# One PSUM bank of the differential attention taken from another pool: the transposed results' bank in a hybrid decoder layer

## The chip, the cores and the metric

The kernel runs on one core of one Trainium2 chip. The metric is the device time of one execution in microseconds; the time of a version is the median of its runs.

## The reference, cut to what matters

One decoder layer on x of 512 tokens by 2048 features, all in float32. A normalised h is multiplied by one wide matrix `w_in`. Its columns feed four heads of gated linear attention (GLA), a gate for them, and four heads of differential attention:

```python
# diff_attention, per head and block of 128 query rows; two score maps c = 0, 1
s = einsum('bqhcd,bkhcd->bhcqk', qi, k) * scale + bias      # ALiBi, causal
p = softmax(s, axis=-1)
a = p[:, :, 0] - lam * p[:, :, 1]
o = einsum('bhqk,bkhe->bqhe', a, v)
# token_mixer
o_b = rmsnorm(o_b, diff_norm) * (1.0 - lambda_init)
return concatenate([o_a, o_b]) @ w_o                         # o_a: the GLA heads, gated
```

Then come a residual, a second norm, and a gated MLP with a causal convolution of width 3 on one branch. `w_in`, `w_o` and the MLP's matrices are what most of the work is spent on.

## The kernel before, in words

**Split products.** Each weight block of 128 x 1024 floats (a granule, `granule`, L128) is loaded, copied by ScalarE into a rounded high half (L137), and VectorE makes the low half by subtraction (L138). Three matmuls per pair of operands (high by high, high by low, low by high) make one product. The halves live in three slots of `ring`.

**Projection units.** `InUnit` (L696) computes one 512-column piece of `w_in` as a block product with seven partial products, the segments x0, z0, y0, z1, x1, y1 and y2. A segment is two granules of 24 matmuls. A segment that begins a sum opens a PSUM bank with `bank(psm)` (L729): x0 opens the bank "y", z0 the bank "z", x1 the bank "x". Bank y stays open from x0 to y2 of its unit, bank z from z0 to z1, bank x for x1 alone. ScalarE or VectorE takes the sums out (L757, L762, L771 and L793 on ScalarE; L776, L782 and L787 on VectorE). The next unit's x0 stands ahead of the old unit's y2, so two banks y can be open at a time. There are ten units (L865 to L872); the last two make the gate of the GLA heads (L810: a product, a sigmoid and another product, L819 to L821, then a store to `ogd`).

**PSUM.** Eight banks of 128 x 512 floats are in two pools of four: `psm` for the block products and `psa` for everything else (L61, L62). `bank()` without an argument takes one of `psa` (L77).

**The attention as filling.** GLA and differential heads are generators. After each granule's products a unit calls `step()` (L84), which advances the first live generator, 0.75 steps per granule. One step i of `diff_heads` (L667 to L688) issues, in this order, for five different blocks of 128 query rows:

- `store(i-5)` (L655): two TensorE transposes of the finished rows `on` into a bank `ob` (L659), a ScalarE copy into `dst` (L661), and a DMA to `dstd`, issued from ScalarE's queue (L662);
- `values(i-3)` (L642): the products with `dvt`, the head's v (L646), then a square on ScalarE (L649), the norm's factor on GpSimd (L144, L146) and the scaled rows `on` on VectorE (L652);
- `fetch_v` of the next head, when a head has ended (L604, one buffer);
- `probs(i)` (L606): two score banks (L614), then VectorE and ScalarE in turn: bias (L616), maximum (L618, L620), exponential (L622), reciprocal (L624, L628), scaling (L629) and difference (L630);
- `turn(i-2)` (L633): transposes of the probabilities into a bank (L637), copied out by ScalarE (L639).

So a step opens five banks of `psa`: one in `store`, one in `values`, two in `probs`, one in `turn`. The rows `jk`, `on` and `dst` share three SBUF buffers (`row_tile`, L339).

**The order.** In this stretch no order is written out by hand. A planner in the framework (Tile) takes the instructions in the order in which the program states them as priorities, simulates the engines, gives each tile a free buffer of its pool and fixes each engine's order; a tile whose buffer is in use makes its first writer wait for the last user. Each engine then runs its own list strictly in that order.

The call sites that drive the attention (`InUnit.run`, L723, calls `step()` at L750) are outside the functions printed here:

```python
            there[after[i - 1][0]] = after[i - 1][1]   # L911: a head's q and k are now there
        pace[0] = 0.75                                   # L913: steps of filling per granule
            drain()                                      # L921: in the last unit, all that is left
```

Of the kernel before, what the change touches and what calls it, by code (L numbers as in the profile page):

```python
# [35 lines left out]
def hybrid_layer(ctx: ExitStack, tc: tile.TileContext, x, attn_pre_norm, w_in, w_alpha_up, b_alpha,  # L36
# [24 lines left out]
    psm = ctx.enter_context(tc.tile_pool(name="psm", bufs=4, space=PSUM))  # L61
# [15 lines left out]
    def bank(pool=None):  # L77
        return (pool or psa).tile([P, 512], F32, name="bank", tag="bank")
# [260 lines left out]
    def row_tile(name):  # L339
        return mx.tile([P, GDV], F32, name=name, tag="jk", bufs=3)  # L340
# [245 lines left out]
    def diff_heads():  # L586
# [67 lines left out]

        def store(n, on):  # L655
            h, qb = divmod(n, NT)
            ob = bank()
            for j in range(2):
                nc.tensor.transpose(ob[:, j * P:(j + 1) * P], on[:, j * P:(j + 1) * P], ident)  # L659
            o = row_tile("dst")  # L660
            act(o, ob[:, :2 * P], AF.Copy)  # L661
            nc.scalar.dma_start(out=dstd[h][:, :, qb * P:(qb + 1) * P], in_=o.rearrange("p (j c) -> p j c", j=2))  # L662
# [4 lines left out]
        for i in range(N + 5):  # L667
            h = i // NT
            if i < N and i % NT == 0:
                while there["diff"] <= h:  # L670
                    yield
                if h not in qs:
                    fetch(h)
                    yield
                    yield
            if i - 5 in summed:
                store(i - 5, summed.pop(i - 5))
            if i - 3 in turned:
                summed[i - 3] = values(i - 3, turned.pop(i - 3))
            if i % NT == 2 and i > NT and h < DH:  # L680
                fetch_v(h)
            if i < N:
                scored[i] = probs(i)
                if i % NT == 3 and h + 1 < there["diff"]:
                    fetch(h + 1)
            if i - 2 in scored:
                turned[i - 2] = turn(i - 2, scored.pop(i - 2))
            yield  # L688
# [968 lines left out]
```

## Time and profile before

| what | value |
|---|---|
| median of 3 runs | 2109.35 us (2107.22 to 2112.05) |
| the profiled execution's own time | 2105.36 us |
| its span, first to last instruction | 2103.7 us |
| mean granted TensorE clock | 0.998 |
| stores of the differential heads (L659) | first at 428.9 us, last at 594.3 us |

The profile gives, per instruction, its engine, its start and its duration; what an engine waited for ahead of it is inferred from semaphores and shown as `[idle <-releaser]`. A row such as `PE bank L637 <- ACT dst L661: 2.3, 2, 1.6` says that TensorE's instructions of line 637, which write a bank, stood waiting 2.3 us in all, 2 times, 1.6 at most, until ScalarE's instruction of line 661, which writes `dst`, had ended. PE is TensorE, PEld its weight loads, ACT ScalarE, DVE VectorE, POOL GpSimd and SP the queue that issues most loads; a `q` behind a name is an engine's instruction queue.

### The profile page before, as it was taken

The page shows a single profiled execution, that of the slowest core. Times are in us where ns is not written, and L with a number is a line of the kernel's source. Part 1 is how long each engine was busy: PE and PEld are TensorE (multiplying, and loading weights), DVE is VectorE, ACT ScalarE, POOL GpSimd, SP SyncE. Part 2 cuts the span into 40 slices and gives each one's busy share as a digit, 9 for nine tenths or more (in the row PEclk, how much of TensorE's full clock was granted, in tenths as well). Part 3 has the DMA queues.
Part 4 walks back from the last instruction along what each step waited for, and adds up shares of the span by engine and source line. Part 5 has one row for each costly group of instructions (what it writes and reads, how often), then busy time and mean ns, then how long its engine had stood idle before and what let it go on. Part 6 is the DMA issues. An engine that isn't in the chain of part 4 may idle for free.

```text
span 2103.7 us, 35572 instructions
## 1 busy us (share of the span) xinstructions
PE 2061.9 (98%) x14449; PEld 1900.6 (90%) x14449; DVE 1508.8 (72%) x1802; ACT 1000.8 (48%) x1306; POOL 286.9 (14%) x306
## 2 busy tenths in 40 slices
PE   7999999999999999999999999999999999999997
PEld 6799999999898889899999999999999878787786
DVE  5967777676662255986777777777777778888877
ACT  4544444455652233454554554555455554444443
POOL 0112122322110000011111111110111111110100
PEclk9999999999999999999999999999999999999999
DMA  5478887878874244448668577667776876775653
GB/s 210 123 185 183 196 184 176 185 172 193 195 201 174 96 151 160 140 102 196 149 149 195 144 162 185 143 159 171 173 160 172 248 210 155 210 184 147 172 168 140
DMA packets 280696, 358.60 MB, mean 170 GB/s; under 512 B 14592, under 2 KB 221876, under 8 KB 278612
## 3 DMA queue, kind: packets, MB, share of 16 engines
q1 hardware_dynamic: 191380, 259.85, 36.9%
q0 software_dynamic: 84800, 94.38, 29.5%
q8 instruction: 113, 1.85, 0.4%
q10 hardware_dynamic: 4352, 2.10, 0.3%
q14 instruction: 51, 0.42, 0.1%
HBM read 311.72 MB, written 44.56 MB: 169 GB/s over the span
## 4 chain that ended last, share of the span: by engine, by line
PE 50%; issue 19%; POOL 2%; DVE 2%; DMA 2%; ACT 1%; POOLq 0%; DVEq 0%; ACTq 0%
PE bank L1247 10%; PE bank L1246 10%; PE bank L1248 10%; PE bank L191 3%; PE bank L193 3%; PE bank L192 3%; PE bank L175 1%; PE bank L173 1%; PE bank L174 1%; PE bank L1349 1%; PE bank L1350 1%; PE bank L1348 1%; POOL rt L1194 1%; POOL raw L1194 1%; PE bank L746 1%
## 5 line engine op out<-in xcount | busy, mean ns | idle before, releaser
L138 DVE TENSOR_TENSOR ring<-raw,ring 128x1024 fp32r<-128x1024 f32 x315 | 383.5, 1222 | 280.7 <-ACT ring L137 280.4
L137 ACT ACTIVATE ring<-raw 128x1024 fp32r<-128x1024 f32 x315 | 333.2, 1060 | 506.8 <-PE bank L1247 110.4
L1246 PE MATMUL bank<-ah,ring 128*128 128x256 f32 x1280 | 353.3, 276 | 0.0
L1248 PE MATMUL bank<-ah,ring 128*128 128x256 f32 x1280 | 353.3, 276 | 0.0
L1247 PE MATMUL bank<-al,ring 128*128 128x256 f32 x1280 | 353.3, 276 | 0.0
L137 ACT ACTIVATE ring<-rt 128x1024 fp32r<-128x1024 f32 x221 | 233.4, 1060 | 252.1 <-PE bank L1247 158.5
L138 DVE TENSOR_TENSOR ring<-rt,ring 128x1024 fp32r<-128x1024 f32 x221 | 269.2, 1222 | 90.3 <-ACT ring L137 90.1
L1247 PEld LDWEIGHTS bank<-al,ring 128*128 128x128 f32 x1280 | 240.2, 188 | 0.1
L1246 PEld LDWEIGHTS bank<-ah,ring 128*128 128x128 f32 x1280 | 240.2, 188 | 0.1
L1248 PEld LDWEIGHTS bank<-ah,ring 128*128 128x128 f32 x1280 | 240.2, 188 | 0.0
L1349 PE MATMUL bank<-ring,ah 128*128 128x512 f32 x424 | 166.3, 392 | 5.6 <-DVE ring L138 5.6
L1350 PE MATMUL bank<-ring,al 128*128 128x512 f32 x424 | 165.2, 390 | 0.0
L1348 PE MATMUL bank<-ring,ah 128*128 128x512 f32 x424 | 159.0, 392 | 1.0 <-ACT ring L137 0.9
L191 PE MATMUL bank<-ring,ah 128*128 128x512 f32 x280 | 109.8, 397 | 1.9 <-ACT ring L137 1.9
L192 PE MATMUL bank<-ring,ah 128*128 128x512 f32 x280 | 110.2, 395 | 0.4 <-DVE ring L138 0.4
L193 PE MATMUL bank<-ring,al 128*128 128x512 f32 x280 | 109.2, 393 | 0.0
L1194 POOL DMA_DIRECT2D raw<-in_w_ffn_in_dram x40 | 51.2, 1308 | 395.0 <-DVE ring L138 395.0
L1349 PEld LDWEIGHTS bank<-ring,ah 128*128 128x128 f32 x424 | 79.6, 188 | 25.8 <-DVE ring L138 9.5
L1348 PEld LDWEIGHTS bank<-ring,ah 128*128 128x128 f32 x424 | 79.2, 188 | 20.2 <-ACT ring L137 3.7
L1194 POOL DMA_DIRECT2D rt<-in_w_ffn_in_dram x40 | 50.9, 1271 | 327.4 <-DVE ring L138 281.8
L1350 PEld LDWEIGHTS bank<-ring,al 128*128 128x128 f32 x424 | 79.6, 188 | 16.3
L746 PE MATMUL bank<-ring,ah 128*128 128x256 f32 x320 | 93.1, 291 | 0.0
(346 smaller groups left out, 5672.4 us busy)
## 6 DMA issues: line engine op xcount, KB each, us to landing
raw<-in_w_ffn_in_dram SPq DMA_DIRECT2D x96, 512.0 KB, 5.0
raw<-in_w_in_dram SPq DMA_DIRECT2D x56, 512.0 KB, 4.7
raw<-in_w_ffn_out_dram SPq DMA_DIRECT2D x48, 512.0 KB, 6.1
raw<-in_w_in_dram POOLq DMA_DIRECT2D x40, 512.0 KB, 7.1
rt<-in_w_ffn_in_dram SPq DMA_DIRECT2D x40, 512.0 KB, 5.5
rt<-in_w_ffn_in_dram POOLq DMA_DIRECT2D x40, 512.0 KB, 6.1
raw<-in_w_ffn_in_dram POOLq DMA_DIRECT2D x40, 512.0 KB, 6.7
raw<-in_w_o_dram SPq DMA_DIRECT2D x32, 512.0 KB, 3.8
```

The lines of the kernel that those rows point to most:

```text
L137: act(hi, raw, AF.Copy)
L138: tt(lo, raw, hi.bitcast(F32), ALU.subtract)
L191: mm(banks[t], ah[:, t, s, :], w[0][:, k, :], start=st, stop=False)
L192: mm(banks[t], ah[:, t, s, :], w[1][:, k, :], start=False, stop=False)
L193: mm(banks[t], al[:, t, s, :], w[0][:, k, :], start=False, stop=sp)
L1194: nc.gpsimd.dma_start(out=raws[g].rearrange("p (a b) -> p a b", a=self.a), in_=self.block(0, j, g), accum_op=ALU.add)
L1246: mm(o, wh, sh[:, :, kk, :], start=start and kk == 0 and n == 0, stop=False, **NOW)
L1247: mm(o, wh, sl[:, :, kk, :], start=False, stop=False, **NOW)
L1248: mm(o, wl, sh[:, :, kk, :], start=False, stop=kk == HK - 1, **NOW)
L1348: mm(b[j], sh[:, o:o + P], w[0][:, q, :], start=start and st == 0, stop=False, **NOW)
L1349: mm(b[j], sh[:, o:o + P], w[1][:, q, :], start=False, stop=False, **NOW)
L1350: mm(b[j], sl[:, o:o + P], w[0][:, q, :], start=False, stop=st == 3, **NOW)
```

## The change

`store` asks for its bank in `psm`, the pool of the block products, in place of `psa`. The transposes, the copy and the DMA are the same instructions. A step of the differential attention now opens four banks of `psa` and one of `psm`.

```diff
         def store(n, on):
             h, qb = divmod(n, NT)
-            ob = bank()
+            ob = bank(psm)
             for j in range(2):
                 nc.tensor.transpose(ob[:, j * P:(j + 1) * P], on[:, j * P:(j + 1) * P], ident)
             o = row_tile("dst")
```

## The prediction

> **What bounds the kernel now.** I read the page first, then the busy time by stage, the waits of the stretch with the stores, and the order of time on each engine where a wait stands.
>
> ```profile
> PE 2061.9 (98%) x14449; PEld 1900.6 (90%) x14449; DVE 1508.8 (72%) x1802; ACT 1000.8 (48%) x1306; POOL 286.9 (14%) x306
> ...
> 429.00:600.00 171.00, 164.84 (x1272) 155.56 (x1271) 109.34 (x200) 96.37 (x183) 38.67 (x47) 0.99 0.82 191
> ```
>
> TensorE is the bound: 98% of the span, and 164.84 of the 171 us from the first store to the last. The change adds and removes no instruction, so all that it can win in its own stretch is TensorE's idle time there, 171.00 - 164.84 = 6.2 us, and a slower clock behind it. Which part of the 6.2 us is a wait for a bank? The waits of 429 to 600 us (total, times, longest):
>
> ```profile
> DVE on L652 <- DMA dstd<-dst: 10.0, 4, 5.2
> ...
> PE bank L637 <- ACT dst L661: 2.3, 2, 1.6
> ...
> PE bank L646 <- DVE nm L620: 2.0, 1, 2.0
> ...
> PE bank L659 <- DVE s L616: 0.9, 1, 0.9
> ...
> PE bank L659 <- ACT aT L639: 0.2, 1, 0.2
> ```
>
> L637 (the transposed probabilities) needs nothing that L661 makes; it waits because L661 empties the store's bank, which is its own next one. L659 (the store) needs neither L616 nor L639; it waits for a score bank and for a transposed one to be emptied. These are the waits of a pool with five openings a step and four banks. In order of time on TensorE:
>
> ```profile
> 492.06 0.55 PE L637 MATMUL bank<-ident,s 128*128 128x128 f32 x3 [0.77 <-ACT dst L661]
> ...
> 544.62 0.55 PE L637 MATMUL bank<-ident,s 128*128 128x128 f32 x3 [1.55 <-ACT dst L661]
> ...
> 547.33 0.44 PE L659 MATMUL bank<-ident,on 128*128 128x128 f32 x2 [0.89 <-DVE s L616]
> ...
> 562.14 0.44 PE L659 MATMUL bank<-ident,on 128*128 128x128 f32 x2 [0.17 <-ACT aT L639]
> ...
> 565.54 0.67 PE L646 MATMUL bank<-dvt,aT 128*128 128x256 f32 x2 [2.01 <-DVE nm L620]
> ```
>
> The last one is named after a VectorE instruction that L646 doesn't need, but another thing ends just then. L646 here begins a new head, whose v was loaded late:
>
> ```profile
> 560.97 0.36 SPq L48 DMA_DIRECT2D ogd<-u  x1
> 561.42 0.57 SPq L48 DMA_DIRECT2D dvt<-dvd  x1
> ...
> dvt<-dvd SPq DMA_DIRECT2D x1, 512.0 KB, 4.0
> ```
>
> Issued at 561.42 and landed 4.0 us later is 565.42; L646 starts at 565.54. I read this wait as the DMA's, not a bank's.
>
> **The change part by part.**
>
> *What goes.* With four openings of `psa` a step, a bank comes round after a full step in place of four fifths of one, and `turn` no longer follows the store's copy. All four bank waits go: 0.77 + 1.55 + 0.89 + 0.17 = 3.38 us. What is late next at 544.62? The probabilities are old by then; behind the transposes the products need their granule's halves.
>
> ```profile
> 543.39 1.23 DVE L138 TENSOR_TENSOR ring<-raw,ring 128x1024 fp32r<-128x1024 f32 x1 [1.75 <-ACT ring L137]
> ...
> 545.93 0.28 PE L748 MATMUL bank<-ring,ah 128*128 128x256 f32 x1
> ```
>
> The low half is there at 543.39 + 1.23 = 544.62. Counting 24 products to a granule from 533.66 on, L748 at 545.93 is the first that uses it; moved up by 1.55 it would come at 544.38, so 0.24 us is given back. Left: 3.14 us.
>
> *What of it is given back later.* The 0.77 at 492 comes ahead of a long run of products without a wait, and I count it in full. The other 1.55 - 0.24 + 0.89 + 0.17 = 2.37 us lie ahead of the wait for v, and are worth something only if v lands earlier too. What sets v? SP issues it behind `ogd<-u`, whose data VectorE finishes at 560.94; that follows from here:
>
> ```profile
> 550.03 0.36 ACT L661 ACTIVATE dst<-bank 128x256 f32<-128x256 f32 x1
> 550.42 0.52 ACTq L662 DMA_DIRECT2D dstd<-dst  x1
> ...
> 554.85 0.48 DVE L652 SCALAR_TENSOR_TENSOR on<-bank,rs,dnb 128x256 f32<-128x256 f32 x1 [2.08 <-DMA dstd<-dst]
> ...
> 555.58 0.68 DVE L787 TENSOR_TENSOR u<-u,bank 128x512 f32<-128x512 f32 x1
> ...
> 560.25 0.69 DVE L821 TENSOR_TENSOR u<-u,op 128x512 f32<-128x512 f32 x1 [1.81 <-ACT u L820]
> ```
>
> VectorE stands 2.08 us until a store's DMA has given back a row buffer, and the unit's emptying (L787), the gate (L819, L820, L821), `ogd<-u` and v queue behind it. The store's transposes at 547.33 + 0.44 were done 2.3 us ahead of its copy at 550.03: the copy stands behind the exponentials in ScalarE's list, which wait for VectorE, not for TensorE. So if ScalarE's order stays, v lands at 565.4 whatever TensorE does, and TensorE waits there 2.01 + 2.37 = 4.4 us. Ends for this part: 0 and 2.37 us won. I take 0, for the row nearest to it (v's issue) says so.
>
> *The clock.* After that wait TensorE is slow:
>
> ```profile
> 562.00:566.00 4.00, 1.84 (x12) 1.64 (x13) 3.75 (x9) 3.30 (x5) 1.41 (x2) 1.00 0.95 305
> 566.00:570.00 4.00, 4.00 (x11) 2.31 (x11) 3.76 (x8) 2.06 (x8) 1.11 (x2) 0.59 0.42 132
> ```
>
> The columns are PE, PEld, DVE, ACT, POOL, then the granted clock. After 4 us with 1.84 busy the clock is 0.59 for 4 us, which costs (1 - 0.59) x 4 = 1.6 us. It is the one such dip from the first store to the last. If the wait shrinks or shifts, these 1.6 us are won; if it grows to 4.4, as much may be lost again. I take 0.
>
> The Trainium skill, "TensorE: Matmul & The Clock Gate", section "Why this matters for your kernels", asks for no idle gap of TensorE above some 3 us. By that rule the 2.01 us here would cost nothing more, and only the longer wait would; the row speaks against it, with a slow clock behind 2.01 us (its section "What's actually happening" has the activity judged over a window that runs freely, which a shorter gap can mostly fill, and that the row allows).
>
> *What is added.* `psm` gets 16 openings, each held from the transposes to the copy's end. What I can see of the four banks:
>
> ```profile
> 435.64 0.38 PE L659 MATMUL bank<-ident,on 128*128 128x128 f32 x2
> ...
> 437.62 0.28 PE L742 MATMUL bank<-ah,ring 128*128 128x256 f32 x1
> ...
> 437.93 0.36 ACT L661 ACTIVATE dst<-bank 128x256 f32<-128x256 f32 x1
> ...
> 438.44 0.69 DVE L776 TENSOR_TENSOR u<-bank,u 128x512 f32<-128x512 f32 x1
> ...
> 594.26 0.41 PE L659 MATMUL bank<-ident,on 128*128 128x128 f32 x2
> ...
> 596.51 0.28 PE L746 MATMUL bank<-ring,ah 128*128 128x256 f32 x1
> ...
> 599.05 0.37 ACT L661 ACTIVATE dst<-bank 128x256 f32<-128x256 f32 x1
> ...
> 599.79 0.68 DVE L776 TENSOR_TENSOR u<-bank,u 128x512 f32<-128x512 f32 x1
> ```
>
> At 437.62 x1 opens a bank while y is open, z isn't emptied until 439.13 and the store's bank would be held until 438.29: the fourth of four. At 596.51 it is the same, the store's held until 599.42 and z until 600.48. Nowhere did I find a fifth, so every opening has a bank that is free. Bounds: 0, and the time that the store's bank is still held where a product opens one: 438.29 - 437.62 = 0.67, 599.42 - 596.51 = 2.91, and a third at 498.59 of 0.32 (below): 3.9 us. Where a wait is added, all products queue behind it on TensorE. I take 0, for free banks are what the rows show.
>
> ```profile
> 498.59 0.47 PE L746 MATMUL bank<-ring,ah 128*128 128x256 f32 x1
> ...
> 498.55 0.36 ACT L661 ACTIVATE dst<-bank 128x256 f32<-128x256 f32 x1
> ```
>
> *Sum.* -0.77 us; against the profiled execution's own time 2105.36 - 0.8 = 2104.6. That run lies 4.0 us under the median, which stands for the kernel, so I put it on the median: 2109.35 - 0.8 = 2108.6.
>
> **The rivals.**
>
> *Faster: the stores move up.* Without a bank of `psa` to wait for, the planner may place L659, and with it L661, ahead of the step's exponentials. Then dst lands earlier, L652's wait (10.0 us in 4 times on VectorE) shrinks, and gate and v come earlier by the 2.08 us. TensorE wins the whole 3.14 us, and the dip of 1.6 us may go: -4.7, 2104.6 us. All idle time and the dip, 6.2 + 1.6 = 7.8, is the end: 2101.5. For it: the 10.0 us are real, and stand on the path to v. Against: in all three of the copies that I show in order (437.93, 550.03, 599.05) ScalarE came late for other reasons than the bank. Chance 0.22.
>
> *Slower: products wait for the store's copy.* If the planner, whose ScalarE may be ahead of the real one, gives an opening product the bank that a store has just left, TensorE stands until L661 has ended. It decides wherever the copy ends later than the product's turn comes, at the three places above: 3.9 us, with one more dip behind the 2.91 of 1.6 us. 3.9 + 1.6 - 0.8 = +4.7: 2114.1 us. For it: copies end up to 599.42 - 594.26 = 5.2 us after their transposes. Against: a fourth bank was free. The Trainium skill, "Perfetto Trace Analysis", section "Matmuls", wants independent groups to rotate through banks so that one is emptied beside the next one's matmuls; a foreign, slowly emptied tenant in that rotation is what it would warn of, and no row here shows one yet. Chance 0.27.
>
> *Nothing happens.* The planner's order stays and L637 finds another bank late, L639's or L616's: 2109.4 us. Chance 0.10, within the same verdict. The forecast itself has 0.41.
>
> **How the numbers follow.** A measurement of this kernel tells about 0.2%, 4.2 us, from no change. Faster: 0.22, and 0.02 of the forecast's tail: 0.24. Slower: 0.27. Same: the rest of the forecast and the case of nothing, 0.49. The range reaches from under the end of the faster case, 2101.5 less 1 us, 2100.5, to 2114.1 and the 2.7 us by which one run of before lay above its median: 2116.8.
>
> **What would show it.** Right: L637 no longer waits for L661, L659 for neither L616 nor L639; no product (L742 to L748) waits for L661; TensorE's wait ahead of the first L646 of the last head is longer than 2.01 us, behind a v that is issued near 561 us less 0.8. The faster rival shows as L661 ahead of L622 in ScalarE's order, less than 10.0 us of L652 waiting for dst, and no dip of the clock. The slower one shows as PE L742 or L746 waiting for ACT L661. I am wrong in the whole if the planner's new order moves time outside 429 to 600 us.

## The result and the profile after

| version | runs | median us | range us | ratio to the kernel before, with interval |
|---|---|---|---|---|
| before | 15 | 2109.20 | 2104.25 to 2114.40 | |
| changed | 15 | 2104.41 | 2100.50 to 2106.97 | 0.9979 (0.9970 to 0.9989) |
| changed, a second time | 12 | 2104.73 | 2100.67 to 2109.07 | 0.9984 (0.9973 to 0.9995) |

The change gains some 0.2%: 4.8 us by the first pair of medians, 2.4 us by the second (before: 2107.17 in 35 runs). That it is faster is clear of the noise in both comparisons; by how much is not, for the two intervals reach from 0.05% to 0.30%. The forecast was 2108.6, a gain of 0.8 us on the 2109.35 of before.

The profiled execution of the changed kernel took 2106.11 us (span 2104.4), 0.75 us *more* than that of before. Single executions of either kernel spread over more than 6 us, so the two profiles show which waits come and go, but not what the median does. First the stretch with the stores and its waits, as before:

```profile
429.00:600.00 171.00, 163.35 (x1269) 155.45 (x1268) 112.71 (x204) 100.05 (x192) 39.65 (x47) 0.99 0.84 198
```

```profile
ACT ah L150 <- DMA dt<-dstd: 9.4, 2, 7.9
...
PE bank L659 <- DVE on L652: 5.7, 1, 5.7
...
DVE on L652 <- DMA dstd<-dst: 1.5, 1, 1.5
...
PE bank L646 <- ACT aT L639: 1.4, 1, 1.4
```

All the waits for a bank are gone: no row of L637 for L661, none of L659 for L616 or L639. VectorE stands for a row buffer 1.5 us in place of 10.0. Yet TensorE is busy for 163.35 us of the 171, less than the 164.84 of before, for new waits have come. The long one is that of the last store for its rows. The shorter one is a wait of 1.4 us of the values product (L646) for the transposed probabilities that ScalarE copies out (`aT`); it ends at 546.56, close to where L637 stood 1.55 us for a bank before (544.62). So part of what the banks gave is taken again by ScalarE. In order of time on TensorE:

```profile
490.33 0.61 PE L614 MATMUL bank<-dk,dq 128*128 128x128 f32 x4
490.77 0.49 PE L637 MATMUL bank<-ident,s 128*128 128x128 f32 x3
...
560.96 0.60 PE L646 MATMUL bank<-dvt,aT 128*128 128x256 f32 x2
...
590.07 0.28 PE L746 MATMUL bank<-ring,in_s3h 128*128 128x256 f32 x1
596.05 0.66 PE L659 MATMUL bank<-ident,on 128*128 128x128 f32 x2 [5.70 <-DVE on L652]
```

Three things are to be seen. `turn` (L637) now stands directly behind the scores (L614); before, products stood between them, 492.06 against 488.61 + 0.61 for the same block. The planner has a free bank earlier and has made another order. The last head's first values product (560.96) has no wait in front of it; its v is issued seven microseconds earlier than the 561.42 of before, SP's list:

```profile
554.23 0.57 SPq L48 DMA_DIRECT2D dvt<-dvd  x1
...
558.20 0.36 SPq L48 DMA_DIRECT2D ogd<-u  x1
...
587.48 0.52 SPq L48 DMA_DIRECT2D dt<-dstd  x1
```

This list has another order as well: v stands ahead of the gate's store `ogd<-u`, behind which it stood before. What its issue now waits for is the earlier head's last values product, which reads the one buffer that v has and ends at 554.20. Among SP's waits from 540 to 570 us:

```profile
SPq L48 <- PE bank L646: 5.8, 1, 5.8
```

The gate's store itself is only 2.8 us earlier, 558.20 in place of 560.97.

And the last store waits 5.70 us. Why, is in ScalarE's list:

```profile
548.76 0.40 ACT L622 ACTIVATE s<-s,nm 128x128 f32<-128x128 f32 x1
...
549.16 0.36 ACT L661 ACTIVATE dst<-bank 128x256 f32<-128x256 f32 x1
549.43 0.39 ACT L622 ACTIVATE s<-s,nm 128x128 f32<-128x128 f32 x1
...
584.82 0.58 ACT L771 ACTIVATE u<-bank 128x512 f32<-128x512 f32 x1
593.34 0.63 ACT L150 ACTIVATE ah<-dt 128x512 fp32r<-128x512 f32 x1 [7.94 <-DMA dt<-dstd]
593.87 0.37 ACT L649 ACTIVATE jk<-bank 128x256 f32<-128x256 f32 x1
```

At 549.16 the store's copy now stands between the two exponentials of a step, no longer behind both. At 585.40, when L771 has ended, ScalarE turns to L150, a split (a rounded high half, by ScalarE, and a low half, by VectorE) of finished attention rows that `place_diff(0)` reads back from `dstd`. The load of those rows is issued at 587.48 and they aren't there until 593.3; ScalarE stands 7.94 us, and behind it in its list stands the square (L649) of the very last block, which GpSimd, VectorE's `on`, the last store, and with it TensorE wait for. In the kernel before, the square came ahead of that split:

```profile
590.12 0.38 ACT L649 ACTIVATE jk<-bank 128x256 f32<-128x256 f32 x1 [2.92 <-PE bank L646]
...
598.52 0.63 ACT L150 ACTIVATE ah<-dt 128x512 fp32r<-128x512 f32 x1 [4.20 <-DMA dt<-dstd]
```

There ScalarE stands 4.20 us for the same load, but the last store's transposes (594.26) are done by then. In the changed kernel the wait also leaves a slow clock (columns as in the prediction):

```profile
588.00:596.00 8.00, 2.35 (x20) 2.14 (x19) 1.18 (x2) 1.98 (x5) 0.88 (x2) 0.95 1.15 297
595.00:602.00 7.00, 5.95 (x28) 5.98 (x29) 4.83 (x6) 3.13 (x4) 0.38 (x1) 0.51 0.91 314
```

For 7 us behind it the clock is 0.51: up to 5.95 x 0.49 = 2.9 us of TensorE's work lost on top of the 5.70.

A wait of before that lies behind 600 us goes, too. It stands ahead of the first product with `w_o`:

```profile
611.58 0.96 PE L191 MATMUL bank<-ring,ah 128*128 128x512 f32 x3 [1.85 <-ACT ring L137]
```

In the changed kernel the same product (612.59) has no wait in front of it.

### The profile page after: what moved, and what is told of

It is laid out like the page before. It is cut to its first block, busy times and chain, and to the rows that moved or that the text cites. A ratio compares the mean times of both kernels' runs of the same rounds, so it can differ in the third digit from the quotient of the medians.

```text
span 2104.4 us, 35571 instructions
## 1 busy us (share of the span) xinstructions
PE 2062.8 (98%) x14449; PEld 1903.4 (90%) x14449; DVE 1507.9 (72%) x1802; ACT 1001.9 (48%) x1306; POOL 287.5 (14%) x306
## 3 DMA queue, kind: packets, MB, share of 16 engines
q8 instruction: 113, 1.85, 0.4%
## 4 chain that ended last, share of the span: by engine, by line
issue 37%; PE 29%; POOL 3%; DMA 2%; DVE 2%; ACT 1%; POOLq 0%; DVEq 0%; ACTq 0%; SPq 0%
PE bank L1248 4%; PE bank L1247 4%; PE bank L1246 4%; PE bank L191 3%; PE bank L192 3%; PE bank L193 3%; POOL raw L1194 1%; POOL rt L1194 1%; PE bank L1349 1%; PE bank L1350 1%; PE bank L1348 1%; PE bank L1553 1%; PE bank L1554 1%; PE bank L1552 1%; PE bank L175 1%
## 5 line engine op out<-in xcount | busy, mean ns | idle before, releaser
L137 ACT ACTIVATE ring<-raw 128x1024 fp32r<-128x1024 f32 x315 | 333.3, 1060 | 516.4 <-PE bank L1247 119.7
L137 ACT ACTIVATE ring<-rt 128x1024 fp32r<-128x1024 f32 x221 | 233.2, 1060 | 247.3 <-PE bank L1247 146.1
```

The source lines that it names most:

```text
L137: act(hi, raw, AF.Copy)
```

## The experiments

My theory after this: moving one of five openings out of a pool of four took the bank waits away and let the whole attention run earlier, and most of that was given back at the last store. The rivals: the time went elsewhere; the store's bank is special, not the count; the products' pool pays.

**Both kernels again**

> The kernel before, a second time, for a second profile. Ratio to before 1.000 within 0.1%. Theory (bank waits): the same four places wait for a bank again, L637 for L661 some 2.3 us in all, L659 some 1 us, and the first values product of the last head waits some 2 us for its v. Rival (the difference of 4.8 us between the medians lies elsewhere, in how often TensorE's clock is halved): the stretch from the first scores to the first product with w_o takes another time than the 209.8 us of the first profile, by 1.7 us for each halving of 3.4 us more or less.

> The changed kernel, a second time. Ratio 0.998. Theory: no wait of L637 for L661 and none of L659 for L616 or L639, v of the last head issued near 554 us as in the first profile, and TensorE's wait of some 5.7 us ahead of the last store with a halved clock behind it again, since ScalarE's and SP's lists are the same. Rival: that last wait was an accident of one execution (a store's DMA that landed late) and is under 2 us here; then the stretch from the first scores to w_o, 208.9 us in the first profile, is 4 to 8 us shorter.

Measured: before 2107.49 us, ratio 1.0000 (0.9991 to 1.0009); changed 0.9984. The waits of TensorE in the stretch, before and then changed:

```profile
PE bank L637 <- ACT dst L661: 2.1, 1, 2.1
PE bank L646 <- DVE mxv L618: 1.8, 1, 1.8
```

```profile
PE bank L659 <- DVE on L652: 5.9, 1, 5.9
...
PE bank L646 <- ACT aT L639: 1.9, 1, 1.9
...
DVE on L652 <- DMA dstd<-dst: 1.5, 1, 1.5
```

My expectation of before failed in part. The last head's wait for v is there again (1.8 us), and so is the one ahead of `w_o` (2.5 us); but of the four places that waited for a bank only one does, L637 near 544 us. Over all profiles of before, those of the runs below included, the waits for a bank come to 2.1 to 3.5 us in one execution, in changing places; the profiles of the changed kernel show none. The wait of its last store belongs to the kernel: 5.9 us here, 5.70 there. The stretch from the first scores to the first product with `w_o` took 209.8 and 209.3 us in the two profiles of before, 208.9 and 210.4 us in those of the changed kernel, so the profiles show no gain in it.

The stretches with a clock near one half, the halvings, don't fall in the same places. In the first profile of before the clock was 1.00 from 544 to 548 us and from 612 to 616, and 0.59 from 566 to 570; in the second:

```profile
544.00:548.00 4.00, 3.75 (x19) 3.75 (x20) 3.97 (x8) 2.95 (x7) 2.25 (x3) 0.57 0.59 169
566.00:570.00 4.00, 4.00 (x28) 3.28 (x27) 4.00 (x10) 1.71 (x7) 1.11 (x2) 1.00 0.47 137
612.00:616.00 4.00, 4.00 (x23) 3.95 (x22) 4.00 (x7) 1.78 (x4) 0.00 (x0) 0.59 0.58 185
```

So (1 - 0.57) x 4 = 1.7 us go with each, and which of the kernel's waits sets one off changes from execution to execution. The first part of the rival holds, then, for single executions: one profile of either kernel is too little to read 3 us from.

**The placing of rows stated later**

```diff
             drain()
-            place_diff(0)
             u.x1()
+            place_diff(0)
             turn_gate(0)
```

> The changed kernel with the first placing of the attention's rows (place_diff(0), its loads of dstd and its splits) stated after the last unit's x1 in place of ahead of it. Theory: the wait ahead of the last store is ScalarE standing on a split (L150) whose load isn't there, with the last block's square behind it; moved back, the wait of 5.7 us and the slow clock of some 3 us behind it go: 4 to 8 us faster than the changed kernel, ratio 0.994 to 0.996. Rival: the last store waits for the chain of the last block itself (square, factor, scaling), whatever the placing: no change against the changed kernel, 0.998.

> The kernel before with the same move of place_diff(0). Theory: before, the splits stood behind the last block's square, so nothing waits for them there that TensorE needs, and only the 1.85 us ahead of w_o can change: 0 to 2 us faster, ratio 0.999 to 1.000. Rival (the move by itself gains, with either pool): 4 to 8 us faster, 0.996 to 0.998.

Measured: changed kernel 2104.58 us, 0.9989 (0.9978 to 0.9999); before 2108.28 us, 1.0003 (0.9990 to 1.0016). The first looks like the rival's result, but the profile says that the question was not put:

```profile
ACT ah L150 <- DMA dt<-dstd: 10.8, 2, 9.1
...
PE bank L659 <- DVE on L652: 6.8, 1, 6.8
```

ScalarE still stands on L150 ahead of the square. The order in which the program states work is only a priority; the planner takes what its simulation holds ready, and presumably it held `dt` ready too early. Moving the statement didn't move the instruction: ScalarE's list is that of the changed kernel.

**The split tied behind**

So I tied it: an ordering edge without a wait, from the halves of the x1 segment to the splits of the last head's rows.

```diff
-        act(hi, raw, AF.Copy)
-        tt(lo, raw, hi.bitcast(F32), ALU.subtract)
+        latest[0] = act(hi, raw, AF.Copy)
+        latest[1] = tt(lo, raw, hi.bitcast(F32), ALU.subtract)
...
-            place_diff(0)
+            place_diff(0, range(3))
             u.x1()
+            with tc.issue_after(latest[0].ins), tc.issue_after(latest[1].ins):
+                place_diff(0, [3])
```

> The changed kernel with one pair of splits tied down: the split of the last head's first rows (L150 on ScalarE, L151 on VectorE, from the load dt of dstd) is issued behind the halves of the last unit's x1 segment, so that ScalarE no longer stands on it ahead of the last block's square (L649). TensorE's own order stays as in the changed kernel, and the kernel before has this order already. Theory: TensorE's wait of 5.7 and 5.9 us ahead of the last store, and the halving of the clock for 6.8 us behind it, go; 5 to 9 us faster than the changed kernel, 2095 to 2100 us, ratio 0.995 to 0.997, and the stretch from the first scores to w_o is 200 to 204 us. Rival (the last store waits for its own chain anyway, or the products of x1 then wait for ScalarE): the wait moves to the next product, ratio 0.998 as the changed kernel.

Measured: 2101.78 us (2095.77 to 2107.32), 0.9975 (0.9963 to 0.9988); the lowest median of all versions. TensorE's list is that of the changed kernel; a few places of ScalarE's, VectorE's and SP's differ. ScalarE, the last store on TensorE, and the clock in the same two windows:

```profile
583.72 0.38 ACT L649 ACTIVATE jk<-bank 128x256 f32<-128x256 f32 x1 [0.81 <-PE bank L646]
...
586.72 1.06 ACT L137 ACTIVATE ring<-raw 128x1024 fp32r<-128x1024 f32 x1 [0.72 <-ACT dst L661]
592.21 0.63 ACT L150 ACTIVATE ah<-dt 128x512 fp32r<-128x512 f32 x1 [4.44 <-DMA dt<-dstd]
```

```profile
587.70 0.38 PE L659 MATMUL bank<-ident,on 128*128 128x128 f32 x2
...
596.00 0.39 PE L746 MATMUL bank<-ring,ah 128*128 128x256 f32 x1 [1.10 <-ACT ring L137]
597.26 0.39 PE L748 MATMUL bank<-ring,ah 128*128 128x256 f32 x1 [0.76 <-DVE ring L138]
```

```profile
588.00:596.00 8.00, 6.90 (x61) 6.66 (x59) 3.04 (x5) 2.01 (x4) 0.00 (x0) 1.00 1.12 326
595.00:602.00 7.00, 5.24 (x43) 5.04 (x44) 5.98 (x8) 5.54 (x8) 0.00 (x0) 1.00 0.94 322
```

The square goes at 583.72, the last store has no wait, the clock stays at 1.00. ScalarE still stands 4.44 us for `dt`, and products then wait 1.10 and 0.76 us for halves: a smaller wait in place of the large one, and part of the rival. The median is 2.6 us under that of the changed kernel in its first comparison, less than the 5 us that I set as the least. By the ratios, 0.9975 against 0.9979 and 0.9984, the whole kernels don't even show that tying gains. One reason is in the profile: the wait ahead of `w_o`, which the changed kernel had lost, is back:

```profile
606.74 0.96 PE L191 MATMUL bank<-ring,ah 128*128 128x512 f32 x3 [2.54 <-ACT ring L137]
```

The gain at the place itself is shown by the cut kernels below.

**Another opening moved**

```diff
-            tb = bank()          # turn, L635
+            tb = bank(psm)
```

with `store` in `psa` as before.

> The kernel before with another of the five openings moved: the transposed probabilities' bank (L635) from the block products' pool, the store's from the attention's pool as before. Theory (it is the count, five openings on four banks, that made the waits): L637 no longer waits for L661, L659 waits for nothing but its rows, v of the last head is issued near 554 us, and the time is that of the changed kernel within 3 us, ratio 0.997 to 1.000. Rival (it matters that it is the store's bank, which is emptied latest): L659 keeps a wait for L616 or L639 of 1 us or more, and the ratio is 1.000 or above.

> The kernel with the transposed probabilities' bank moved in place of the store's, whole, a second time. Theory: its bank waits are gone as in the changed kernel and other waits stand in their place (a product for its halves, near 573 and 602 us): 1.000 within 0.1% again, and the same two places wait in its profile. Rival: those waits were an accident of one execution, and the ratio is 0.998 to 0.999.

(The second run bears a label of the cut kernels, but is the whole kernel.) Measured: 2108.71 us, 1.0002 (0.9990 to 1.0014), and 2108.89 us, 1.0005 (0.9993 to 1.0017). Of the first:

```profile
552.01 0.57 SPq L48 DMA_DIRECT2D dvt<-dvd  x1
```

```profile
PE bank L748 <- DVE ring L138: 2.6, 2, 1.9
...
PE bank L746 <- ACT ring L137: 2.3, 1, 2.3
PE bank L646 <- DVE s L616: 2.0, 1, 2.0
...
PE bank L659 <- ACT dst L661: 0.3, 1, 0.3
```

As to the waits the count is what matters: L637 no longer waits for L661, the store waits 0.3 us for a bank (0.8 in the second profile), and v is issued at 552.01. The 2.0 us of L646 are named after a score bank's reader, L616, but its `aT` is there only at 543.79 + 0.47 = 544.26 (L639) and it starts at 544.70, so a bank can have cost at most 0.44 us of them. As to the time, my expectation failed: products now wait 2.6 and 2.3 us for their halves (2.7 and 2.2 in the second profile), and nothing is won. Fewer waits for banks are worth what the planner's new order lets through.

**A bank of the products' pool kept occupied**

```diff
-    there["gla"] = 2
+    there["gla"], held_bank = 2, bank(psm)
+    nc.tensor.transpose(held_bank[:, :P], ident, ident)
...
             drain()
+            nc.vector.tensor_copy(tmp("held")[:, :P], held_bank[:, :P])
```

> The changed kernel with one bank of the products' pool kept occupied from the first scores to the end of the attention (a transposed identity is put in it and read out at the end, one instruction of TensorE and one of VectorE more). Products and stores have three banks. Theory of the slower rival: at the three openings where the fourth bank was the free one, products or stores now wait for a copy, 1 to 4 us in all, and the planner may put stores later; 0 to 6 us slower than the changed kernel, ratio 0.998 to 1.001. Rival (products never need more than two banks beside the store's): no wait of a product for L661, ratio as the changed kernel.

> The kernel before with the same bank kept occupied: the control of the run with three banks. Products alone never held more than three banks in the profile of before, so no product waits for a bank: ratio 1.000 within 0.1%, and the four waits for a bank of the attention's pool (L637 for L661, L659 for L616 and L639) stay.

Measured: changed kernel 2107.90 us, 1.0000 (0.9990 to 1.0010); before 2108.06 us, 1.0003 (0.9990 to 1.0015). With three banks for products and stores the change gains nothing; products alone need no fourth. But the price isn't a product that waits for a copy:

```profile
PE bank L659 <- DVE on L652: 5.5, 1, 5.5
...
PE bank L646 <- DMA dvt<-dvd: 2.5, 1, 2.5
...
PE bank L659 <- DVE p L782: 0.3, 1, 0.3
```

One store waits 0.3 us for x to be emptied (L782). No product waits for a bank. The rest sits in another order again, with a wait of 2.5 us for an earlier head's v; the control speaks for the missing bank as the cause, but by what path it acts is not shown, and the interval (from 0.9990) still touches that of the changed kernel's second comparison (to 0.9995).

**The front part alone**

To take the later spread out, three kernels end behind three quarters of the product with `w_o`. TensorE's list up to there is that of the whole kernel. Close to the first product with `w_o` the others are not quite: SP issues two small loads earlier, and one of the splits L150 has moved behind the first halves of `w_o` (L137).

```diff
     for c in range(3):
         proj_n(w_o3, 512 * c, lambda t, b, c=c: evac_m(c, t, b), order)
+    for t in range(NT):
+        dma(out2[t * P:(t + 1) * P, 0:1536], m[t][:, 0:1536])
+        dma(out2[t * P:(t + 1) * P, 1536:2048], m[t][:, 0:512])
```

> The kernel before, cut off behind the third of four column blocks of the product with w_o: the rest of that product, the residual, the norm and the whole MLP are left out, and what stands in m is written out. Up to there every engine's list is that of the kernel before. It is the base of the four cut kernels: some 800 to 815 us, with a spread of 1 to 2 us, as only the halvings of the clock in this part are left.

> The changed kernel, cut at the same place; lists as in the changed kernel up to there. Theory (the gain of some 3 us is made in the attention's stretch: the waits for banks and for v that go, with the halvings behind them, are worth 3 us more than the wait ahead of the last store that comes): 2 to 4 us less than the kernel before cut. Rival (the profiles of the stretch are right, 209.4 us on average with either; the gain comes later): within 1 us of it.

> The changed kernel with the pair of splits tied behind x1, cut at the same place. Theory: 5 to 7 us less than the kernel before cut and 3 to 5 less than the changed kernel cut, as the stretch in its profile (204.7 us) says. Rival (its gain is spread over the kernel): under 3 us less than the kernel before cut.

| cut kernel | runs | median us | range us |
|---|---|---|---|
| before | 5 | 757.52 | 755.69 to 759.51 |
| changed | 4 | 756.58 | 755.16 to 757.46 |
| changed, split tied behind | 4 | 751.34 | 750.66 to 751.98 |

(I had expected 800 to 815 us for the base.) The changed kernel wins 0.9 us in this part, with ranges that overlap: closer to the rival than to my 2 to 4 us. Tied behind, it wins 6.2 us over before and 5.2 over the changed kernel, with ranges apart, as the theory of the last store said.

The split that has moved makes these differences other than those of the whole kernels. ScalarE ahead of `w_o`, in the kernel before whole and then cut:

```profile
609.95 0.63 ACT L150 ACTIVATE ah<-dt 128x512 fp32r<-128x512 f32 x1 [1.81 <-DMA dt<-dstd]
610.49 1.04 ACT L137 ACTIVATE ring<-raw 128x1024 fp32r<-128x1024 f32 x1
```

```profile
608.06 0.63 ACT L150 ACTIVATE ah<-dt 128x512 fp32r<-128x512 f32 x1 [0.28 <-DMA dt<-dstd]
608.60 1.04 ACT L137 ACTIVATE ring<-raw 128x1024 fp32r<-128x1024 f32 x1
```

Whole, the halves of `w_o` stand behind a split that waits for its rows, and that makes TensorE's wait of 1.85 us at 611.58; the four profiles of whole kernels with no opening moved (the first two of before, the placing stated later, the occupied bank) show 1.85 to 2.8 us there. Cut, the first product with `w_o` has no wait. The changed kernel has none, whole or cut, and the tied one 2.54 us whole, 1.19 cut. So the cut kernels leave out a wait of some 2 us that the change removes from the whole kernel, and their gain of the tied split over the changed kernel is, by these two profiles, some 1.4 us too good.

TensorE's busy time in the stretch, cut kernels in that order:

```profile
429.00:600.00 171.00, 164.71 (x1261) 155.79 (x1260) 108.90 (x197) 95.25 (x182) 37.06 (x46) 0.98 0.81 189
```

```profile
429.00:600.00 171.00, 163.98 (x1270) 156.07 (x1268) 112.36 (x201) 99.32 (x186) 38.77 (x47) 0.98 0.84 201
```

```profile
429.00:600.00 171.00, 168.48 (x1316) 160.25 (x1315) 114.94 (x204) 100.78 (x189) 37.56 (x47) 0.99 0.83 200
```

The count behind TensorE's busy time is its matmuls in this window: 1261, 1270 and 1316.

## Why the prediction was right and where it failed

- **The bound and the bank waits: right.** TensorE's idle time was where to look, and the waits read as a pool with five openings and four banks went; the run with `turn` moved shows nearly the same of another opening. The 3.38 us were those of one execution (others: 2.1 to 3.5 us), and counting them as won overlooked L646, which waits 1.3 to 1.9 us for ScalarE's copy `aT` in each profile of the changed kernel, cut and with the placing stated later included.
- **"If ScalarE's order stays, v lands at 565.4 whatever TensorE does": the condition failed.** I took 0 of 2.37 us because of it. The planner put the store's copy between the exponentials, VectorE's wait for row buffers fell from 10.0 to 1.5 us, and the gate's store came 2.8 us earlier. By these signs the rival "the stores move up" is what happened, and not the forecast. But v came seven microseconds earlier, at 554.23, by a way that neither had: SP's new list no longer has it behind the gate's store.
- **That rival's price: wrong, and so was the list of what is late next.** That the median of 2104.41 lies beside its 2104.6 is luck. Much of what was won was given back at a place that I had not looked at, the end of the attention, where the new order lets ScalarE stand on a split ahead of the last block's square: 5.70 us and a slow clock. With that one pair tied behind, the cut front part wins 6.2 us, between the 4.7 us and the 7.8 us that I had set as the end.
- **The sum, -0.8 us: too small for the whole kernel (2.4 to 4.8 us), and near the -0.9 us of the cut kernels by luck.** It was not that nothing came of the 2.37 us, but that more came and was lost again; and the cut kernels leave out the wait ahead of `w_o`.
- **My sign of being wrong in the whole came true.** The new order did move time outside 429 to 600 us: the wait of before ahead of `w_o` went, at 611.58, and the slow clock behind the last store reached to 602 us.
- **The slower rival: no product ever waited for the store's copy.** A fourth bank was free, as the rows said; in the run without it the gain was gone.
- **The clock: the price was right** (1.6 us forecast, 1.7 from the row). That I took 0 for it missed that the wait which sets a halving off changes from run to run, so no single profile gives its term.
- **The rest is open.** The whole kernel gains 2.4 to 4.8 us by medians, the cut front part 0.9. From the first product with `w_o` on, TensorE's, ScalarE's and GpSimd's lists are the same in both kernels. For the remaining 2 us or so the wait ahead of `w_o` is a candidate, with the halving behind it (612 to 616 us in the second profile of before). That it is the cause isn't shown: the part from that product on took 1492.1 and 1492.2 us in the profiles of before, 1491.8 and 1489.7 us in those of the changed kernel, but 1495.6 us in that of before with the placing stated later, whose order there is the same. Nor is it shown what the bank waits and v's new place in SP's list are worth each by itself.

## What to carry to other kernels

Count a pipeline step's openings against its pool: one more than there are banks shows as TensorE waiting for a copy that its instruction doesn't need, and moving one opening to a pool with a free bank took all or nearly all of those waits away, for both openings that were tried. That is not yet time: where a planner makes the lists, it makes all of them anew, and the gain must be looked for up to the end of the stretch, above all where an engine's list has an instruction waiting for a DMA ahead of one that the bound engine needs. To move such an instruction, tie it; stating it later may change nothing. And a kernel cut short gets lists of its own near the cut: compare them before its times.

## What the runs showed of the hardware

TensorE's clock falls to half behind waits shorter than I had thought, and not behind all of them. In the first profile of before a wait of 2.01 us was followed by 4 us at 0.59, one of 1.55 us by none; in the second profile one of 2.1 us at the earlier place was followed by 4 us at 0.57. The 5.70 us of the changed kernel led to 7 us at 0.51. Taken over the 14 profiles of these kernels, from 425 to 625 us: none of the seven waits of TensorE of 1.3 to 1.85 us was followed by a halving, that is, by one that began during it or within 2.4 us of its end; of the 21 waits of 1.87 to 2.81 us 15 had one, of 3.4 us each, and six, among them those of 2.54 and 2.81 us, had none; all five of 5.5 to 6.8 us had one of 6.8 us. The Trainium skill, "TensorE: Matmul & The Clock Gate", section "What's actually happening", has the activity judged in freely running windows of 3.4 us, which agrees with the 3.4 us of a halving here, and with halvings that come and go between executions of one kernel; the 3 us of its section "Why this matters for your kernels", as the longest gap to allow, is too much for these runs, where gaps from 1.87 us on were followed by a halving.
